# A two-block diffusion transformer on one core: modulation dealt out in single operations, w2 asked for earlier, a new order of the first steps

## The chip, the cores and the metric

The kernel runs on one core of a Trainium2 chip. The metric is the device time of one execution in microseconds (us), as the median of several. The core has a matrix engine (TensorE; in the profile PE for its products and PEld for its weight loads), a vector engine (VectorE, DVE), a scalar engine (ScalarE, ACT), GpSimd (POOL, unused here but for four constants) and SyncE (SP), which issues most of the DMA transfers. Each engine works through its own queue in order.

## The reference

256 latent tokens (`x`) and 256 context tokens (`ctx`), each 1024 wide, pass two blocks. Block 0 mixes by a short convolution, block 1 by grouped-query attention. Each block has an FFN, the mixer and a second FFN; each of the three reads a modulated norm and adds its gated result. The modulation vectors come from one product of `silu(c)` with a 1024 x 9216 matrix per block. Everything is fp32.

```python
def _modulate(t, g, shift, scale):
    return _rms(t, g) * (1 + scale) + shift

def _swiglu(h, w13, w2):
    gte, up = jnp.split(h @ w13, 2, axis=-1)
    return (jax.nn.silu(gte) * up) @ w2

for i in range(DEPTH):          # DEPTH = 2, FFN_HIDDEN = 2816
    mod = (silu(c) @ mod_w[i] + mod_b[i]).reshape(bsz, 3, 3, 1, D_MODEL)
    modc = (silu(c_ctx) @ mod_w[i] + mod_b[i]).reshape(3, 3, D_MODEL)
    lat = lat + 0.5 * mod[:, 0, 2] * _swiglu(_modulate(lat, norm_g[i, 0], mod[:, 0, 0], mod[:, 0, 1]),
                                             ffn_w13[i, 0], ffn_w2[i, 0])
    # the context the same way with modc; then the mixer (convolution or attention) on both,
    # gated by mod[:, 1, 2]; then the second FFN, gated by mod[:, 2, 2].
    # In block 1 the context only serves keys and values: its second FFN falls away.
```

## The kernel before

**Layout and arithmetic.** Activations lie transposed: 1024 features as 8 tiles (k) of 128 partitions, and 512 tokens as columns, the latents (s = 0) and the context (s = 1) with 256 each. Each operand is split into a high part that the matrix engine takes exactly and a low remainder (`split`, L90 to L92: ScalarE writes the high part, VectorE subtracts). `mm3` (L111) makes three products for one: high by high, high by low, low by high (lines L115, L116, L117).

**FFN.** `ffn` (L571) cuts the 22 tiles of the hidden width into thirds of 8, 7 and 7. For each hidden tile of a third a `Pair` (L496) computes gate and up with seven products of half size in place of eight (a Strassen scheme), which needs sums of the weights (VectorE) and sums of the activations, called T1 to T4 (`sums`). Then `project` (L433) multiplies the third's hidden tiles by w2 for 8 output tiles m, and `finish` (L412) adds each to x, times a gate. The first three tiles of a projection are begun before the last hidden tile is ready (`between`). After the last third, `tail_norm` computes the next norm. In the page the weight splits of w13 and w2 are `wh` and `wl`, the products of a pair `p` and `q`, those of a projection `py`.

**The modulation.** All but the first chapters of it are dot products on VectorE (L138, tile `junk`): one instruction multiplies a 128 x 1024 tile of the transposed matrix with one broadcast vector and sums it up. There are 72 chapters-by-quarters in all; `jobs` lists 64 blocks in the order in which they are wanted (chapter ch of block l, quarter `pair`). One `mod_job` loads 1 MB (`wr<-in_modT`) and runs four such instructions (two tiles by two vectors; two instructions for the last chapters of block 1, where the context is no longer read). `tick(share)` adds a share to `owed` and runs that many whole jobs; it is called after each `finish` in a projection (ev = 0.5, in the third FFN 0.9), and after each tile of the convolution (1.2). `mod_ready(l, ch)` runs at once whatever is missing for a chapter: a gate is asked for at a projection's first `finish` (`lazy_gate`), shift and scale at the norm behind the last tile, and everything left after the third FFN (L829), ahead of the q projections.

**What sets the order.** Nothing in the code is a queue of its own. A planner at build time takes the instructions in the order of the code as their priority, and puts on each engine the first one that is ready and has its buffers by its own estimate of the time; the order found is then fixed. Buffers that matter: three raw weight buffers of 1 MB (`wr`, L86), used by all weights and by the modulation alike; four pairs of split halves (`wh`, `wl`, L97); six PSUM tiles for products.

**The first block.** At the start nothing is there but x. `FIRST_STEPS` (L31) is a hand-written order of steps: W (load and split one w13 tile; three of them), P (`mod_pe`: a quarter of shift, ch 0, or scale, ch 1, of the first norm on TensorE from a separately laid out 1 MB of `mod0`), D (`mod_dve`: such a quarter on VectorE), S (load the broadcast vectors), N (the norm of two k tiles), M (the products of one w13 tile with two k tiles). Five quarters go through P and three through D. In a P step 8 products move 256 matrix columns past a 2-column stationary operand, the 2-row result is copied by ScalarE (L683), and two small products turn it (L685). Only after all steps come `h.sums()` and the three `w13_post` (silu, product, split).

Of the kernel before, what the change touches and what calls it, by code (L numbers as in the profile page):

```python
# [9 lines left out]
F32 = mybir.dt.float32  # L10
# [6 lines left out]
P = 128  # L17
# [20 lines left out]
def hybrid_kernel(ctx: ExitStack, tc: tile.TileContext, a: dict, out: bass.AP):  # L38
# [90 lines left out]
    def mod_job(l, ch, pair):  # L129
        mt = mod_tile(l, ch)  # L130
        nv = 1 if (l == 1 and ch >= 5) else 2
        raw = load_raw(a["modT"][l, ch * 4 + pair])
        for j in range(2):
            kt = pair * 2 + j
            col = ch * KT + kt
            for v in range(nv):
                junk = mp.tile([P, D], BF16, name=nm("junk"), tag="junk", bufs=1)
                nc.vector.tensor_tensor_reduce(  # L138
                    out=junk,
                    in0=raw[:, j * D : j * D + D],  # L140
                    in1=scbc[:, v, :],
                    scale=1.0,
                    scalar=modb[:, l, col : col + 1],
                    op0=ALU.mult,
                    op1=ALU.add,
                    accum_out=mt[:, kt, v : v + 1],
                )
        done[l, ch] += 1

    jobs = [(0, ch, p) for ch in range(2, 9) for p in range(4)]  # L150
    jobs += [(1, ch, p) for ch in range(9) for p in range(4)]
    owed = [0.0]

    def tick(share):

        owed[0] += share
        while jobs and owed[0] >= 1:
# [107 lines left out]
    class Blocks:  # L265
# [45 lines left out]
    class FirstBlocks(Blocks):  # L311
# [13 lines left out]
        def sums(self):  # L325
            r = self.raw
            tt = nc.vector.tensor_tensor
            for key in ("T1", "T2", "T3", "T4"):
                self.t[key] = hot("th"), hot("tl")
# [6 lines left out]
            b = lambda hf, s, q: r[2 * hf + q, s]  # L336
            for q in range(2):
# [779 lines left out]
```

## Time and profile before

| what | value |
|---|---|
| median of 3 runs | 1635.54 us (1632.44 to 1636.04) |
| the profiled execution's own time | 1636.17 us |
| its span, first to last instruction | 1634.1 us |
| mean granted TensorE clock | 0.984 of full |
| PE / PEld / DVE / ACT busy | 1581.4 / 1463.5 / 1358.5 / 735.1 us |
| modulation on VectorE (L138) | 236 instructions, 302.4 us |
| DMA | 248.81 MB, mean 152 GB/s |

The page gives for each engine its busy time and for groups of instructions the count, the mean duration and the idle time before them with what ended it. Queries of the trace give the same for any stretch of time, with the clock granted to TensorE in it (1.00 is full speed), the chain of work that ended last, and each queue's DMA issues. A busy TensorE isn't TensorE at its peak, so prices are taken from start to start or from counts in a stretch.

### The profile page before, as it was taken

The page shows a single profiled execution, that of the slowest core. Times are in us where ns is not written, and L with a number is a line of the kernel's source. Part 1 is how long each engine was busy: PE and PEld are TensorE (multiplying, and loading weights), DVE is VectorE, ACT ScalarE, POOL GpSimd, SP SyncE. Part 2 cuts the span into 40 slices and gives each one's busy share as a digit, 9 for nine tenths or more (in the row PEclk, how much of TensorE's full clock was granted, in tenths as well). Part 3 has the DMA queues.
Part 4 walks back from the last instruction along what each step waited for, and adds up shares of the span by engine and source line. Part 5 has one row for each costly group of instructions (what it writes and reads, how often), then busy time and mean ns, then how long its engine had stood idle before and what let it go on. Part 6 is the DMA issues. An engine that isn't in the chain of part 4 may idle for free.

```text
span 1634.1 us, 26052 instructions
## 1 busy us (share of the span) xinstructions
PE 1581.4 (97%) x10746; PEld 1463.5 (90%) x10746; DVE 1358.5 (83%) x2066; ACT 735.1 (45%) x1131; POOL 0.2 (0%) x4
## 2 busy tenths in 40 slices
PE   9898999999999999999999999989999989999999
PEld 6697898998888889989899889789899879899999
DVE  4999998889988979898898989999898978756454
ACT  5552352554322356435245465235255346554443
POOL 0000000000000000000000000000000000000000
PEclk9999999999999999999999999999999989999999
DMA  8335525334445513452433513552633742245453
GB/s 317 132 106 189 195 98 189 114 124 174 150 171 187 188 52 104 155 180 97 163 141 116 182 52 109 185 197 97 247 136 126 270 172 94 78 146 190 168 186 112
DMA packets 38279, 248.81 MB, mean 152 GB/s; under 512 B 5136, under 2 KB 6928, under 8 KB 12304
## 3 DMA queue, kind: packets, MB, share of 16 engines
q1 hardware_dynamic: 35712, 245.38, 42.9%
q10 hardware_dynamic: 2448, 1.76, 0.4%
q8 instruction: 84, 1.38, 0.3%
q14 instruction: 35, 0.29, 0.0%
HBM read 244.77 MB, written 1.05 MB: 150 GB/s over the span
## 4 chain that ended last, share of the span: by engine, by line
PE 85%; DVE 10%; DMA 2%; ACT 1%; issue 1%; DVEq 0%; ACTq 0%; SPq 0%
PE py L115 8%; PE py L117 8%; PE py L116 8%; PE p L117 7%; PE p L115 7%; PE p L116 7%; PE q L117 5%; PE q L115 5%; PE q L116 5%; DVE junk L138 4%; DVE wl L92 2%; PE pg L116 2%; PE pg L115 2%; PE pg L117 2%; PE pu L116 2%; PE pu L117 2%
## 5 line engine op out<-in xcount | busy, mean ns | idle before, releaser
L91 ACT ACTIVATE wh<-wr 128x1024 fp32r<-128x1024 f32 (+2 forms) x269 | 269.9, 1013 | 401.6 <-PE py L116 92.2
L92 DVE TENSOR_TENSOR wl<-wr,wh 128x1024 fp32r<-128x1024 f32 (+2 forms) x269 | 311.5, 1165 | 103.0 <-ACT wh L91 102.4
L138 DVE CUSTOM_DVE_ANT_0 junk<-wr,scbc,modb 128x1024 bf16<-128x1024 f32 x236 | 302.4, 1281 | 28.1 <-DMA wr<-in_modT 25.4
L117 PE MATMUL py<-gh,wl 128*128 128x512 f32 (+1 forms) x746 | 264.0, 355 | 5.9 <-DVE wl L92 5.9
L115 PE MATMUL py<-gh,wh 128*128 128x512 f32 (+1 forms) x746 | 265.2, 355 | 4.6 <-ACT wh L91 4.6
L116 PE MATMUL py<-gl,wh 128*128 128x512 f32 (+1 forms) x746 | 265.1, 355 | 0.0
L92 DVE TENSOR_TENSOR wl<-ws,wh 128x1024 fp32r<-128x1024 f32 x122 | 148.7, 1223 | 30.0 <-ACT wh L91 29.7
L117 PEld LDWEIGHTS py<-gh,wl 128*128 128x128 f32 x746 | 142.0, 190 | 26.7 <-DVE wl L92 7.3
L91 ACT ACTIVATE wh<-ws 128x1024 fp32r<-128x1024 f32 x122 | 128.3, 1058 | 81.9 <-PE p L116 37.6
L115 PEld LDWEIGHTS py<-gh,wh 128*128 128x128 f32 x746 | 142.3, 191 | 24.1 <-ACT wh L91 5.7
L116 PEld LDWEIGHTS py<-gl,wh 128*128 128x128 f32 x746 | 142.2, 191 | 18.3
L116 PE MATMUL p<-tl,wh 128*128 128x256 f32 x488 | 138.2, 283 | 0.0
L115 PE MATMUL p<-th,wh 128*128 128x256 f32 x488 | 138.2, 283 | 0.0
L117 PE MATMUL p<-th,wl 128*128 128x256 f32 x488 | 137.8, 283 | 0.0
L115 PE MATMUL q<-bh,wh 128*128 128x256 f32 x336 | 95.2, 283 | 0.4 <-ACT gm L551 0.4
L116 PE MATMUL q<-bl,wh 128*128 128x256 f32 x336 | 95.2, 283 | 0.0
L117 PE MATMUL q<-bh,wl 128*128 128x256 f32 x336 | 95.1, 283 | 0.0
L116 PEld LDWEIGHTS p<-tl,wh 128*128 128x128 f32 x488 | 93.8, 192 | 0.3
L115 PEld LDWEIGHTS p<-th,wh 128*128 128x128 f32 x488 | 93.8, 192 | 0.3
L117 PEld LDWEIGHTS p<-th,wl 128*128 128x128 f32 x488 | 93.5, 192 | 0.0
L417 DVE SCALAR_TENSOR_TENSOR x<-py,G,x 128x256 f32<-128x256 f32 x168 | 73.6, 479 | 22.0 <-PE py L117 21.7
L91 ACT ACTIVATE gh<-gm 128x512 fp32r<-128x512 f32 (+1 forms) x88 | 50.7, 576 | 62.7 <-DVE gm L568 52.9
(234 smaller groups left out, 4073.5 us busy)
## 6 DMA issues: line engine op xcount, KB each, us to landing
wr<-in_w SPq DMA_DIRECT2D x88, 1024.0 KB, 4.9
wr<-in_modT SPq DMA_DIRECT2D x67, 1024.0 KB, 5.0
wr<-in_w2b SPq DMA_DIRECT2D x32, 896.0 KB, 4.6
wr<-in_w2a SPq DMA_DIRECT2D x16, 1024.0 KB, 4.8
wr<-in_cw_cx SPq DMA_DIRECT2D x8, 1024.0 KB, 4.9
wr<-in_mod SPq DMA_DIRECT2D x5, 1024.0 KB, 7.9
wr<-in_cw_b SPq DMA_DIRECT2D x4, 1024.0 KB, 4.9
wr<-in_cw_out SPq DMA_DIRECT2D x4, 1024.0 KB, 5.0
```

The source lines that it names most:

```text
L91: nc.scalar.activation(out=hi, in_=src, func=AF.Copy)
L92: nc.vector.tensor_tensor(out=lo, in0=src, in1=hi.bitcast(F32), op=ALU.subtract)
L115: nc.tensor.matmul(ps, wh, mh, start=first, stop=False, **kw)
L116: nc.tensor.matmul(ps, wh, ml, start=False, stop=False, **kw)
L117: nc.tensor.matmul(ps, wl, mh, start=False, stop=last, **kw)
L138: nc.vector.tensor_tensor_reduce(out=junk, in0=raw[:, j * D : j * D + D], in1=scbc[:, v, :], scale=1.0, scalar=modb[:, l, col : col + 1], ...
L417: nc.vector.scalar_tensor_tensor(out=x[:, m, s * S : s * S + S], in0=ps[:, o : o + S], scalar=g[:, m, s : s + 1], in1=x[:, m, s * S : s * ...
```

## The change

1. `FIRST_STEPS` is reordered. All eight quarters of the first norm's modulation go through P; D is gone. P turns its product round: 128 x 128 pieces of the matrix are the stationary operand and the 2 columns of silu(c) are moved, so the result comes out in place, without the copy and the turning products. New steps: T (one of four parts of the activation sums, `part`), F (`w13_post` of one of the first three tiles), and U (one single modulation operation), eight of them.
2. A unit of the modulation is now one VectorE instruction (`mod_unit`); `next_unit` loads a new block when the last one's units are used up. `tick(n)` counts units: 1.5 per `finish` in the first two FFNs and in the fourth, where none is left, 2 in the third, 5 per tile of the convolution, 1 in its output projection; new is `ev13`, 1.6 after each pair in the first third of the first FFN. `mod_ready` fills up as before, in units.
3. In `project` each call for w2's tile m also asks for m + 1 and m + 2 (`get`).
4. `block(fine=True)` writes the high part straight from the norm and the low part from the same source; the fp32 copy comes after.

```diff
 FIRST_STEPS = (
-    "W0 P11 P10 P00 N0 P01 N1 P12 W1 S M00 M10 M01 M11 D02 N2 M02 D13 W2 D03 M12 M20 M21 N3 "
-    "M03 M22 M13 M23"
+    "P10 P00 W0 N0 P11 P01 N1 W1 S M00 M10 M01 P12 P02 M11 T0 W2 N2 M20 M02 P13 P03 M21 T1 M12 "
+    "N3 T2 M22 M03 F0 T3 M13 F1 U U U U M23 F2 U U U U"
 )
...
+    def next_unit():
+        if not units:
+            l, ch, pair = jobs.pop(0)
+            mod_tile(l, ch)
+            raw = load_raw(a["modT"][l, ch * 4 + pair])
+            units.extend(
+                (l, ch, pair, raw, j, v) for j in range(2) for v in range(streams(l, ch))
+            )
+        mod_unit(*units.pop(0))
+
+    def tick(n):
+
+        owed[0] += n
+        while (jobs or units) and owed[0] >= 1:
             owed[0] -= 1
-            mod_job(*jobs.pop(0))
+            next_unit()
 
     def mod_ready(l, ch):
-        while not ((l, ch) in done and done[l, ch] == 4):
-            mod_job(*jobs.pop(0))
+        while not ((l, ch) in done and done[l, ch] == 8 * streams(l, ch)):
+            next_unit()
         return modv[l, ch]
...
-                nc.scalar.activation(
-                    out=raw[:, c], in_=t, func=AF.Identity, bias=B[:, k, s : s + 1]
-                )
-                if fine and i % 2:
-                    c = slice((i - 1) * S, (i + 1) * S)
-                    split(hi[:, c], lo[:, c], raw[:, c])
+                b = B[:, k, s : s + 1]
+                if fine:
+                    nc.scalar.activation(out=hi[:, c], in_=t, func=AF.Identity, bias=b)
+                    nc.vector.scalar_tensor_tensor(
+                        out=lo[:, c], in0=t, scalar=b, in1=hi[:, c].bitcast(F32),
+                        op0=ALU.add, op1=ALU.subtract,
+                    )
+                nc.scalar.activation(out=raw[:, c], in_=t, func=AF.Identity, bias=b)
...
-        def sums(self):
+        def part(self, n):
...
+            q = n % 2
+            b11, b12, b21, b22 = (r.get((2 * hf + q, s)) for hf in range(2) for s in range(2))
+            if n < 2:
+                tt(out=b11, in0=b12, in1=b11, op=ALU.subtract)
+                keep("T1", q, b11)
+                return
+            tt(out=b12, in0=b22, in1=b12, op=ALU.add)
+            tt(out=b22, in0=b22, in1=b11, op=ALU.add)
+            keep("T2", q, b22)
+            tt(out=b21, in0=b21, in1=b22, op=ALU.subtract)
+            keep("T3", q, b12)
+            keep("T4", q, b21)
...
-        w2 = [ws(m) for m in range(nf)]
+        ahead = {}
+
+        def get(m):
+            for i in range(m, min(m + 3, KT)):
+                if i not in ahead:
+                    ahead[i] = ws(i)
+            return ahead[m]
+
+        w2 = [get(m) for m in range(nf)]
...
-    def ffn(l, b, h, tot, gate, tail, gs=(), ev=0.5):
+    def ffn(l, b, h, tot, gate, tail, gs=(), ev=1.5, ev13=0):
...
                     prev = pr
+                    if t == 0:
+                        tick(ev13)
...
-        for k in range(KT):
-            nc.tensor.matmul(
-                pr[:2, :S], sccol[:, k, :], raw[:, k * S : k * S + S],
-                start=(k == 0), stop=(k == KT - 1),
-            )
-        row = tp.tile([P, S], F32, name=nm("row"), tag="t", bufs=3)
-        nc.scalar.copy(row[:2, :], pr[:2, :S])
         for j in range(2):
-            nc.tensor.matmul(
-                pr[:, S + 2 * j : S + 2 * j + 2], row[:2, j * P : j * P + P], ident[:2, :2],
-                start=True, stop=True,
-            )
+            for k in range(KT):
+                o = k * S + j * P
+                nc.tensor.matmul(
+                    pr[:, 2 * j : 2 * j + 2], raw[:, o : o + P], sccol[:, k, :],
+                    start=(k == 0), stop=(k == KT - 1),
+                )
...
-    ffn(0, 0, h, T2, lazy_gate(0, 0), tail_norm(0, 1, hn), gs0)
+    ffn(0, 0, h, T2, lazy_gate(0, 0), tail_norm(0, 1, hn), gs0, 1.5, 1.6)
...
-        tick(1.2)
+        tick(5)
...
-        lazy_gate(0, 1), tail_norm(0, 2, hn), T2, 2, 0.5,
+        lazy_gate(0, 1), tail_norm(0, 2, hn), T2, 2, 1,
...
-    ffn(1, 0, h, T2, lazy_gate(1, 0), tail_norm(1, 1, hn), (), 0.9)
+    ffn(1, 0, h, T2, lazy_gate(1, 0), tail_norm(1, 1, hn), (), 2)
```

More of the change, by code (lines that the diff above doesn't have):

```diff
@@ L328, in sums @@
             for key in ("T1", "T2", "T3", "T4"):
-                self.t[key] = hot("th"), hot("tl")
+                if key not in self.t:
+                    self.t[key] = hot("th"), hot("tl")
             def keep(key, q, src):
@@ L462, in project @@
                 ready()
-            w = ws(m)
+            w = get(m)
             ps = psum("py")
@@ L468, in project @@
         if late:
-            wl = [ws(m) for m in (6, 7)]
+            wl = [get(m) for m in (6, 7)]
             if tail:
@@ L691, in mod_pe @@
             out=(A00 if ch else B00)[:, k2, :],
-            in0=pr[:, S : S + 4].rearrange("p (k v) -> p k v", v=2),
+            in0=pr[:, :4].rearrange("p (k v) -> p k v", v=2),
             in1=both(sb1[:, k2] if ch else modb[:, 0, k2]),
@@ L745, in hybrid_kernel @@
         steps[step[0]](*(int(c) for c in step[1:]))
-    done[0, 0] = done[0, 1] = 4
-    h = FirstBlocks(h, h32)
-    h.sums()
-    for i in range(3):
-        gs0.append(new_pair("g"))
-        w13_post(pps[i], gs0[i], 0, T2)
+    done[0, 0] = done[0, 1] = 16
+    h = hb
     convk = cload("convk", [P, 3, KT])
```

67 lines of the change are left out of this document (24 added, 43 removed).

## The prediction

> **What bounds the kernel now.** I read the page's totals first, then the granted clock and the busy time by stretches, then the chain of waits, and the DMA issues of SyncE's queue.
>
> ```profile
> span 1634.1 us, 26052 instructions
> PE 1581.4 (97%) x10746; PEld 1463.5 (90%) x10746; DVE 1358.5 (83%) x2066; ACT 735.1 (45%) x1131; POOL 0.2 (0%) x4
> wr<-in_modT SPq DMA_DIRECT2D x67, 1024.0 KB, 5.0
> ```
>
> TensorE is busy 97% of the span. A change can win only where TensorE waits or runs slowly, so I look for these places by stretches (us, then per engine busy time and instructions, then the clock granted):
>
> ```profile
> core 0: us, PE busy (x) PEld busy (x) DVE busy (x) ACT busy (x) POOL busy (x), PEclk, DMA share, GB/s
> 74.50:82.30 7.80, 2.79 (x15) 2.55 (x14) 7.80 (x12) 2.64 (x5) 0.00 (x0) 0.78 0.00 0
> 82.30:129.80 47.50, 47.50 (x385) 47.50 (x385) 42.28 (x52) 27.87 (x42) 0.00 (x0) 0.96 0.34 114
> 129.80:188.50 58.70, 51.53 (x231) 41.91 (x230) 56.68 (x93) 9.16 (x11) 0.00 (x0) 0.91 0.56 200
> 673.90:720.30 46.40, 46.40 (x217) 38.89 (x217) 46.15 (x74) 11.28 (x13) 0.00 (x0) 1.00 0.61 212
> 1027.90:1084.00 56.10, 49.19 (x223) 40.38 (x221) 55.03 (x91) 9.15 (x11) 0.00 (x0) 0.97 0.57 204
> 1300.00:1336.00 36.00, 27.44 (x170) 26.02 (x170) 30.73 (x62) 17.46 (x32) 0.00 (x0) 0.81 0.54 190
> 690.00:716.00 26.00, 26.00 (x116) 21.55 (x115) 25.86 (x42) 6.23 (x7) 0.00 (x0) 1.00 0.60 215
> 100.00:120.00 20.00, 20.00 (x169) 20.00 (x168) 18.79 (x25) 11.31 (x19) 0.00 (x0) 1.00 0.31 106
> ```
>
> The last two rows give TensorE's prices when nothing waits: 26/116 = 0.224 us for a product of 512 columns, 20/169 = 0.118 us for one of 256. The rows before show where it does wait: behind the first block (74.5 to 82.3), in the first w2 projection of the first and third FFN (58.7 and 56.1 us, where the same projection in the second FFN took 46.4), and around the first q projections (1300 to 1336). In the two slow projections VectorE is busy almost throughout, and this is with what (modulation operations alone):
>
> ```profile
> 129.80:188.50 58.70, 39.73 (x31) 0.91 0.56 200
> 673.90:720.30 46.40, 24.33 (x19) 1.00 0.61 212
> 1027.90:1084.00 56.10, 38.58 (x31) 0.97 0.57 204
> ```
>
> One single operation takes 24.33/19 = 1.28 us. With 19 of them a projection runs freely; 12 more cost 58.7 - 46.4 = 12.3 us in one place and 9.7 in the other, so about 0.8 to 1.0 us for each one above 20.
>
> **The modulation, counted from the code.** Before, the first projections get 32, 20 and 32 singles: forced at the first gate 4 blocks, 1 and 1 (a block is four singles on one 1 MB load), ticked 4, 4 and 7. After, 16 singles are done before the first FFN's projection (8 by U, 8 by the ticks of 1.6 in its pair loop), and the ticks then add 12, 40 in the convolution, 6 in its output projection. That leaves 96 where 112 are due at the second FFN's first gate: 16 are forced there, 12 ticked, 28 in all. At the third FFN 145 stand against 160: 15 forced (3 on a block already loaded), 16 ticked, so 28 on new loads. At the end 204 of 224 are done and 20 are forced, in 10 loads, because the last chapters use one stream; before it was 4 loads with 8.
>
> *First FFN's projection*: 12 singles, below 20, so it runs like 673.9: -12.3 us. *Second*: 8 above 20: 8 x 0.8 to 1.0 = +7 (from 0, if the slack behind 20 takes them, to 12, if the early w2 block also keeps a third raw buffer from the modulation, whose loads then queue behind it on SyncE, and with them the gate that the first finish reads; I take the rows' slope). *Third*: the same 28, against 9.7 lost now: -2.5 (from -9.7 to +3). *First FFN's pair loop*: VectorE has 1.2 us free in 20 (18.79 busy), about 0.6 in a pair of 10 us, and gets 1.6 x 1.28 = 2.0: five pairs lack 7 us. The projection that follows absorbs most: +2 (0 to 7).
>
> **The first block.** Before, a P step takes TensorE 4.1 us: 16 records of 256 columns and 4 that turn the row.
>
> ```profile
> 16.46 4.48 PE pr L678 x20
> 20.94 0.53 PE pr L685 x4
> 21.47 3.54 PE pr L678 x16
> ```
>
> After, a P step has 16 products, each with 128 columns of fp32 weights and 2 columns moved, which show as two records each, so 32. Such products are in the trace with one column, in the norm's sums (the first two rows, at clock 1.00) and in the attention's (the last two, at 0.50):
>
> ```profile
> 12.25 0.36 PE L212 MATMUL ss<-ones,sq 128*128 128x1 f32 x2
> ...
> 13.81 0.58 PE L223 MATMUL ss<-ident,ri 128*128 128x128 f32 x3
> 1327.02 1.70 PE L840 MATMUL pqs<-ones,sq 128*128 128x1 f32 x8
> 1328.58 0.77 PE L115 MATMUL pk<-hh,wh 128*128 128x512 f32 x1
> ```
>
> Between start and start these are 14 records in 1.56 us, 0.111 each, and 8 in 1.56 us, 0.195 each. A new P step is then 3.6 us at the full clock and 6.2 at half. Which one holds?
>
> ```profile
> 1324.74:1328.15 3.41, 3.41 (x18) 3.41 (x18) 3.41 (x8) 2.52 (x5) 0.00 (x0) 0.50 0.14 37
> 1328.15:1331.57 3.42, 3.42 (x13) 3.03 (x14) 3.42 (x8) 1.85 (x3) 0.00 (x0) 0.50 0.71 217
> 1331.57:1334.98 3.41, 3.41 (x30) 3.41 (x30) 3.20 (x6) 1.06 (x1) 0.00 (x0) 1.00 0.33 139
> 1433.97:1437.38 3.41, 1.54 (x10) 1.26 (x10) 2.07 (x5) 0.80 (x3) 0.00 (x0) 1.00 0.27 46
> 1437.38:1440.79 3.41, 2.77 (x13) 2.77 (x14) 3.41 (x10) 2.28 (x6) 0.00 (x0) 0.50 0.66 269
> ```
>
> In the first row TensorE is busy all 3.41 us and still isn't granted the full clock for the next 3.42; 1.1 us of that row are the one-column products. After the second row, nearly all wide products, it is granted. So a weight load with a column or two behind it seems not to count as work for the clock. A P step is nothing else, and four stand in a row at the start, two and two later. Against this speaks only that the clock stayed at 1.00 after the 1.56 us of such products at 12.25, but wide warm-up products filled the rest there. I take the half clock as likelier, two to one. The Trainium skill (TensorE: Matmul & The Clock Gate, Part 1) says that the clock falls after an idle stretch of about 3.4 us and follows how busy the engine is. Read as idle time alone, it keeps the new P steps at full clock, and the sum would be rival 1's 1631; the row at 1324.74, busy and not granted, does not agree with that reading.
>
> Sum to the end of the block's products: P starts at about 15 (the row at 13.81), not 16.5. At half clock some 2.7 of the 8 steps still run at full (the first, and the start of each later run): 2.7 x 3.6 + 5.3 x 6.2 = 42.6; 12 M steps of 12 products x 0.224 = 32.3; three restarts in which wide products run at half clock for a stretch, 2 us lost each: 6. The end is at 15 + 80.9 = 95.9. VectorE, 12 singles lighter there (15 us), has the pairs' weights by then, so the 7.8 us of mostly idle time at 74.5 go; pairs run from 95.9 where they ran freely from 82.3: **+13.6**. At full clock: 15 + 28.8 + 32.3 + about 1 waiting for a mod0 load = 77: -5. Five row copies on ScalarE and three tiny additions go, off the path. SyncE asks for eight mod0 blocks where it asked for five and three modT: the same bytes.
>
> **The end of the third FFN.** SyncE's queue there, before (issue, time over all, count):
>
> ```profile
> 1253.60 15.10 SPq L87 DMA_DIRECT2D wr<-in_modT  x4
> 1269.70 0.33 SPq L87 DMA_DIRECT2D wr<-in_w2b  x1
> 1272.23 4.70 SPq L87 DMA_DIRECT2D wr<-in_modT  x2
> 1286.92 0.33 SPq L87 DMA_DIRECT2D wr<-in_w2b  x1
> 1288.63 11.36 SPq L87 DMA_DIRECT2D wr<-in_modT  x4
> 1303.26 12.38 SPq L87 DMA_DIRECT2D wr<-in_wq  x2
> ```
>
> The q weights stand behind the last modulation loads, and the chain goes through them:
>
> ```profile
> 1303.26 5.68 DMA wr<-in_wq
> ...
> 1314.14 0.58 PE pq L117
> ```
>
> Six more loads at (11.36 - 0.33)/3 = 3.7 us are 22 us; the hole of 10 us before 1286.92 takes some 4 of it, since the w2 block is asked sooner. Wq lands 18 us later, at 1327, and the first q products start at 1328 in place of 1314. Of these 14 us some 8 come back: TensorE is busy only 27.4 of the 36 us to 1336, and the second wq, now 12 us behind the first, will follow at once. **+6** (0 if the loads find room in the projection, 16 if nothing comes back).
>
> **Edits taken at nothing.** W2 asked two tiles ahead: the planner already places a load as soon as a buffer is free, so it changes the order against the modulation loads only, counted above; between tiles VectorE's total decides, not w2. Without that cover it could win the longest wait for a w2 tile (total, times, longest), which lies in the first FFN's 12.3:
>
> ```profile
> PE py L115 <- ACT wh L91: 4.6, 1, 4.6
> ```
>
> The fine split writes hi at once and adds 0.5 us of ScalarE per operand beside running products: 0 (-2 to +2). T and F steps are the same instructions earlier; behind the last M they cost 7.8 us today, counted above.
>
> **Sum**, on the profiled execution's own 1636.2 us, which is 0.6 above the median of the three: first block +13.6, its projection -12.3, pair loop +2, second FFN +7, third -2.5, end +6: +13.8, so **1650**.
>
> **Rivals.** *1: the clock stays full in the P steps.* One mechanism, 18.6 us at the first block: 1650 - 18.6 = 1631, faster. It decides as soon as 13.8 of the 18.6 us don't come. For it: the clock after 12.25; against it: the row at 1324.74. *2: VectorE's forced singles find cover.* The planner brings them forward, second FFN +0, end +0, third -9.7: 1650 - 20 = 1630. Against it: singles need loads, and the three raw buffers hold pair weights until the last pair; for it: 20 cost nothing. *3: the q weights come later still, with nothing recovered*: 1650 + 10 = 1660. *4: the early w2 order isn't what the planner makes of it*: no time changes, since I priced it at none.
>
> **How the numbers follow.** Forecast with rival 4: 0.56, its own range 1638 to 1661. Rival 1: 0.28 (of it 0.18 faster, 0.05 the same, 0.05 slower, as the bursts cost). Rival 2: 0.06. Rival 3: 0.10. A change of 0.2% is about what a measurement of this kernel can tell. Faster: 0.18 + 0.06 = 0.24. Same: 0.05 + 0.03 of the forecast's low edge = 0.08. Slower: the rest, 0.68. The range reaches down to 1627, below rivals 1 and 2, and up to 1662.
>
> **What would show it.** Half clock granted between about 17 and 40 us, and P steps of 6 us there; the first products of the pair loop near 96; the first FFN's projection in 46 to 48 us with clock 1.00; idle TensorE at the end of the second FFN's first projection; wq issued near 1320 plus the shift. The prediction is wrong if the clock stays at 1.00 through the first 80 us, or if the second projection and the q weights show no longer waits.

## The result: 1697.1 us, 3.9% slower

The changed kernel takes 1697.12 us (median, 1694.58 to 1702.27) where the kernel before takes 1634.82; the ratio is 1.0387, with a 95% interval from 1.0358 to 1.0416. The forecast was 1650, at most 1662. The direction was right, the size was not.

The page of the changed kernel, its span and its totals:

```profile
span 1692.8 us, 26324 instructions
...
PE 1613.9 (95%) x10902; PEld 1504.7 (89%) x10902; DVE 1348.2 (80%) x2048; ACT 736.3 (43%) x1130; POOL 0.2 (0%) x4
...
PEclk6689999999999999989999999989999969999999
```

The span grew by 58.7 us, though VectorE is 10 us less busy. The clock row (40 slices of the span, tenths of full speed) has two deep holes: the first three slices and one at 1354 to 1396. The same stretches as in the forecast, now of the changed kernel (us, busy time and instructions of each engine, clock granted): the first block's products, the pair loop behind it, the first w2 projections of the first, second and third FFN, and the time ahead of the q products.

```profile
core 0: us, PE busy (x) PEld busy (x) DVE busy (x) ACT busy (x) POOL busy (x), PEclk, DMA share, GB/s
31.40:108.47 77.07, 74.29 (x337) 65.77 (x337) 33.62 (x69) 27.27 (x53) 0.00 (x0) 0.71 0.40 137
108.47:167.97 59.50, 51.25 (x397) 49.81 (x396) 59.33 (x83) 29.58 (x46) 0.00 (x0) 0.94 0.42 146
167.97:214.44 46.47, 46.47 (x218) 38.92 (x217) 40.85 (x62) 11.05 (x13) 0.00 (x0) 1.00 0.57 199
701.10:755.50 54.40, 49.85 (x218) 40.52 (x218) 49.39 (x81) 8.68 (x11) 0.00 (x0) 0.94 0.54 191
1066.40:1117.00 50.60, 48.39 (x219) 39.97 (x218) 45.38 (x76) 8.56 (x10) 0.00 (x0) 0.97 0.54 194
1340.00:1380.00 40.00, 9.06 (x52) 8.10 (x52) 38.82 (x78) 12.25 (x24) 0.00 (x0) 0.61 0.75 258
```

And the modulation's single operations in three of them:

```profile
701.10:755.50 54.40, 34.62 (x27) 0.94 0.54 191
1340.00:1380.00 40.00, 23.87 (x19) 0.61 0.75 258
167.97:214.44 46.47, 15.38 (x12) 1.00 0.57 199
```

The first FFN's projection (167.97) runs freely with 12 singles, as forecast. The second FFN's (701.10) has 27 and loses time. At 1340 TensorE works 9 us of 40, at a clock of 0.61, while VectorE is busy 38.8 us, 23.9 of them with singles.

The shift of the same products between the two traces (start after minus start before) shows where the 58.7 us arise; beside it what the forecast's terms give for that place:

| place | forecast | measured |
|---|---|---|
| first product of the first w2 projection | +15.6 | +38.1 |
| behind that projection | +3.3 | +25.9 |
| second FFN, start of the first projection | +3.3 | +27.2 |
| second FFN, start of the second projection | +10.3 | +39.8 |
| third FFN, start of the last projection | +7.8 | +38.6 |
| first product of the attention scores | +13.8 | +58.8 |
| last product | +13.8 | +58.6 |

Three places lose more than was thought: the first block with its pair loop (22.5 us more), the second FFN (5.6 more, and only half of the 2.5 comes back in the third), and the end of the third FFN (14.2 more).

**The first block, read in the trace.** TensorE's queue at the start (start, us, line, output and operands, count, idle time before it and who ended it):

```profile
13.91 13.26 PE L704 MATMUL pr<-sccol,wr 128*128 128x2 f32 x64
31.40 0.80 PE L116 MATMUL pg<-hh,wh 128*128 128x512 f32 x1 [4.23 <-ACT wh L92]
...
33.27 6.82 PE L704 MATMUL pr<-sccol,wr 128*128 128x2 f32 x32
...
40.53 0.63 PE L118 MATMUL pu<-hh,wl 128*128 128x512 f32 x1
40.95 0.63 PE L116 MATMUL pg<-hh,wh 128*128 128x512 f32 x1
```

Two P steps (64 records) take 13.26 us without a gap, and the clock granted falls to half at 14.47 and comes back at 55.43. The wide products in between cost 0.42 us from start to start, not 0.224. Counted so over the first block as a whole (13.91 to 108.47), the P steps take 45.1 us, the 144 wide products 42.5, idle time 7.0.

The fall itself is not the work of the new P: it comes 0.56 us after the first P product. In e7, one of the runs below, the P steps are the old ones and start at 16.93; there the clock falls at 14.50 too, but it is back as soon as P's wide products have filled a stretch (by the columns above):

```profile
14.50:17.91 3.41, 0.98 (x3) 0.37 (x4) 2.58 (x4) 2.36 (x6) 0.00 (x0) 0.50 0.88 334
17.91:21.32 3.41, 3.41 (x10) 1.03 (x8) 0.00 (x0) 0.00 (x0) 0.00 (x0) 0.50 0.85 293
21.32:24.73 3.41, 3.41 (x19) 1.51 (x17) 0.33 (x2) 0.36 (x1) 0.00 (x0) 1.00 0.45 132
```

What the new P does is to keep the clock down.

**The pair loop.** Behind the block's last product TensorE waits once for 6.3 us, for the low half of a weight that VectorE writes. The longest of TensorE's waits from 104 to 128 us (engine, line, waited for, total, times, longest):

```profile
PE p L118 <- DVE wl L93: 6.3, 1, 6.3
```

What VectorE did meanwhile, until it wrote `wl` (start, us, line, output and operands):

```profile
111.12 1.28 DVE L136 CUSTOM_DVE_ANT_0 junk<-wr,scbc,modb 128x1024 bf16<-128x1024 f32 x1
...
112.93 1.28 DVE L136 CUSTOM_DVE_ANT_0 junk<-wr,scbc,modb 128x1024 bf16<-128x1024 f32 x1
...
114.14 1.23 DVE L93 TENSOR_TENSOR wl<-wr,wh 128x1024 fp32r<-128x1024 f32 x1
```

The singles of the U steps stand in front of the weight that TensorE waits for.

**The end of the third FFN.** SyncE's queue there (issue, time over all, count):

```profile
1317.04 0.33 SPq L88 DMA_DIRECT2D wr<-in_w2b  x1
1322.58 45.56 SPq L88 DMA_DIRECT2D wr<-in_modT  x12
1371.01 3.53 SPq L88 DMA_DIRECT2D wr<-in_wq  x2
```

The chain that ended last, in order of time (start, us, piece):

```profile
1374.58 1.20 DVE junk L136
1376.08 1.29 DVE junk L136
1377.38 1.15 DVE wl L93
1378.58 0.58 PE pq L118
```

Twelve modulation loads stand ahead of the q weights, and the last singles ahead of the first q weight's low half. It is not the loads themselves that set their distance of 4 us. From 1320 to 1372 SyncE waits most of the time for a single on VectorE (L136) that still reads the raw buffer (who waited for whom, total, times, longest):

```profile
SPq L88 <- DVE mod L136: 42.9, 11, 10.0
```

So the queue goes at VectorE's pace. Wq is asked for at 1371.0; with the shift of 38.6 that stood before this place it would have been 1341.9.

### The profile page after: what moved, and what is told of

The parts are those of the page before. It is cut to its first block, busy times and chain, and to the rows that moved or that the text cites. A ratio compares the mean times of both kernels' runs of the same rounds, so it can differ in the third digit from the quotient of the medians.

```text
span 1692.8 us, 26324 instructions
## 1 busy us (share of the span) xinstructions
PE 1613.9 (95%) x10902; PEld 1504.7 (89%) x10902; DVE 1348.2 (80%) x2048; ACT 736.3 (43%) x1130; POOL 0.2 (0%) x4
## 4 chain that ended last, share of the span: by engine, by line
PE 88%; DVE 9%; ACT 2%; issue 1%; DVEq 0%; ACTq 0%
PE py L118 9%; PE py L116 9%; PE py L117 9%; PE p L118 7%; PE p L116 7%; PE p L117 7%; PE q L118 5%; PE q L116 5%; PE q L117 5%; DVE junk L136 4%; PE pr L704 3%; PE pg L116 2%; PE pg L117 2%; PE pu L117 2%; PE pu L118 2%; PE pu L116 2%
## 5 line engine op out<-in xcount | busy, mean ns | idle before, releaser
L136 DVE CUSTOM_DVE_ANT_0 junk<-wr,scbc,modb 128x1024 bf16<-128x1024 f32 x224 | 287.3, 1282 | 17.8 <-DMA wr<-in_modT 15.7
L93 DVE TENSOR_TENSOR wl<-ws,wh 128x1024 fp32r<-128x1024 f32 x122 | 149.0, 1223 | 30.2 <-ACT wh L92 30.1
L116 PEld LDWEIGHTS py<-gh,wh 128*128 128x128 f32 x746 | 142.3, 191 | 21.1 <-ACT wh L92 2.5
```

The costliest lines, as they stand in the source:

```text
L93: nc.vector.tensor_tensor(out=lo, in0=src, in1=hi.bitcast(F32), op=ALU.subtract)
L116: nc.tensor.matmul(ps, wh, mh, start=first, stop=False, **kw)
L136: nc.vector.tensor_tensor_reduce(out=junk, in0=raw[:, j * D : j * D + D], in1=scbc[:, v, :], scale=1.0, scalar=modb[:, l, col : col + 1], ...
```

## The experiments

Times are medians in us. Each row also has the shift of the same products against the kernel before, from the profiles, at the places used above.

| run | us | first w2 projection | behind it | second FFN, first projection | its second projection | third FFN, last projection | scores |
|---|---|---|---|---|---|---|---|
| the changed kernel | 1697.1 | +38.1 | +25.9 | +27.2 | +39.8 | +38.6 | +58.8 |
| e1_old_p | 1671.2 | +7.7 | -4.5 | -2.8 | +9.9 | +15.7 | +35.8 |
| e2_first_old | 1667.5 | +9.9 | -2.3 | -0.2 | +12.8 | +13.7 | +34.7 |
| e3_dealt | 1664.1 | +40.4 | +28.2 | +30.1 | +30.1 | +38.0 | +28.7 |
| e4_no_ahead | 1690.6 | +38.7 | +26.5 | +27.5 | +37.5 | +34.1 | +52.5 |
| e5_filler | 1681.6 | +27.1 | +14.9 | +16.6 | +29.3 | +26.7 | +47.5 |
| e6_old_p_dealt | 1615.2 | +4.2 | -8.0 | -6.4 | -6.4 | -10.8 | -21.7 |
| e7_before_dealt | 1621.6 | +0.8 | -5.3 | -0.5 | -0.5 | -2.7 | -12.3 |
| e8_one_load | 1688.2 | +37.0 | +24.8 | +26.0 | +39.8 | +41.1 | +53.6 |
| e9_no_last | 1664.0 | +43.2 | +31.0 | +32.2 | +44.8 | +43.7 | +31.2 |
| e10_before_new_p | 1651.4 | +16.4 | +16.3 | +16.2 | +16.2 | +15.9 | +15.5 |
| e11_dealt_ahead | 1630.9 | +5.2 | -7.0 | -4.9 | -4.9 | +3.0 | -7.7 |
| e12_no_u | 1678.1 | +29.0 | +18.1 | +20.1 | +21.1 | +22.6 | +42.4 |
| e13_best_no_u | 1611.3 | +5.1 | -7.0 | -6.7 | -6.7 | -8.6 | -22.2 |
| e14_old_fine | 1696.1 | +37.3 | +25.1 | +26.0 | +38.9 | +39.0 | +58.6 |

### e1: the old P step

```diff
-        for j in range(2):
-            for k in range(KT):
-                o = k * S + j * P
-                nc.tensor.matmul(pr[:, 2 * j : 2 * j + 2], raw[:, o : o + P], sccol[:, k, :], ...)
+        for k in range(KT):
+            nc.tensor.matmul(pr[:2, :S], sccol[:, k, :], raw[:, k * S : k * S + S], ...)
+        row = tp.tile([P, S], F32, name=nm("row"), tag="t", bufs=3)
+        nc.scalar.copy(row[:2, :], pr[:2, :S])
+        for j in range(2):
+            nc.tensor.matmul(pr[:, S + 2 * j : S + 2 * j + 2], row[:2, j * P : j * P + P], ident[:2, :2], ...)
```

> The changed kernel with one edit undone: a P step is the old one again (2-column stationary operand, 256 matrix columns moved, the row copied and turned). Order of the steps, U, T, F and all dealing stay. Theory 1 (the new form of P costs time at half clock and leaves the next products cold): the clock stays at 1.00 from 17 to 60 us, a P step takes about 4.1 us in place of 6.4, no wide products run cold, the first product of the pair loop comes at 84 to 90 us where the changed kernel has 108.5; about 1677 us. Rival (the block waits for its loads, each mod0 load behind a raw buffer that a P step frees): the pair loop still begins later than 100, 1690 or more.

1671.2 us (ratio to before 1.0226, 1.021 to 1.0243). The pair loop begins at 84.3, the first w2 projection 30.4 us sooner than in the changed kernel. The block and the pair loop of this run:

```profile
13.86:84.25 70.39, 68.97 (x309) 41.88 (x309) 45.43 (x92) 35.33 (x72) 0.00 (x0) 0.98 0.60 217
84.25:137.60 53.35, 50.54 (x398) 49.40 (x397) 51.47 (x70) 29.06 (x45) 0.00 (x0) 0.97 0.37 134
```

The clock is 0.98 in the block, and the wide products take 33.9 us where they took 42.5. So the form of P is the largest part of the block's loss, and the loads aren't: they follow the P steps that free their buffers. With the old P, the new order and the dealing together leave the kernel 4.5 us ahead of the one before once the first w2 projection is over.

### e2: the first block as before

```diff
-    "P10 P00 W0 N0 P11 P01 N1 W1 S M00 M10 M01 P12 P02 M11 T0 W2 N2 M20 M02 P13 P03 M21 T1 M12 "
-    "N3 T2 M22 M03 F0 T3 M13 F1 U U U U M23 F2 U U U U"
+    "W0 P11 P10 P00 N0 P01 N1 P12 W1 S M00 M10 M01 M11 D02 N2 M02 D13 W2 D03 M12 M20 M21 N3 "
+    "M03 M22 M13 M23 T0 T1 T2 T3 F0 F1 F2 U U U U U U U U"
```

Beside it the old P and the three D steps.

> The changed kernel with the old order of the first steps, the old P and the three D steps; T, F and the eight U follow behind the last M step, so that the count of singles dealt later is that of the changed kernel. Theory 1 (the first block's order and its P steps carry the +38 us at the pair loop): the pair loop begins within 5 us of the kernel before, the first products of the w2 projection come 5 to 15 us late in place of 38 (the eight U and the ticks of 1.6 load VectorE in the pair loop); 1664 to 1675. Rival (the U and the ticks in the pair loop carry most of it): the w2 projection still begins 25 us late or more, 1685 or more.

1667.5 us. The pair loop begins as in the kernel before (74.8), and the w2 projection +9.9 late, with 16 singles in the pair loop. The projection gives back 12.2 for it. This run has the old P, as e1 has, so it doesn't tell the form of P from the order. Beside e1 it says that the old order on top of the old P is worth only another 3.7 us.

### e3: no forced singles

```diff
-    ffn(0, 0, h, T2, lazy_gate(0, 0), tail_norm(0, 1, hn), gs0, 1.5, 1.6)
+    ffn(0, 0, h, T2, lazy_gate(0, 0), tail_norm(0, 1, hn), gs0, 2, 1.6)
-        tick(5)
+        tick(6)
-    ffn(0, 1, h, T2, lazy_gate(0, 2), tail_norm(1, 0, hn), ())
+    ffn(0, 1, h, T2, lazy_gate(0, 2), tail_norm(1, 0, hn), (), 2.5)
-    ffn(1, 0, h, T2, lazy_gate(1, 0), tail_norm(1, 1, hn), (), 2)
+    ffn(1, 0, h, T2, lazy_gate(1, 0), tail_norm(1, 1, hn), (), 2.5)
```

> The changed kernel with higher ticks, so that no single is forced at the second and third FFN's first gate nor ahead of the q projections: 2 per finish in the first FFN (1.5 before), 6 per tile of the convolution (5), 2.5 in the second and third FFN (1.5 and 2). Theory 1 (the forced singles, 28 in the second FFN's first projection and 20 in 10 loads ahead of the q weights, carry the +12.6 and the +20.3): the second projection gives back 8 to 12, the end 12 to 20, the third FFN 0 to 8; 1660 to 1677. Rival (w2 asked two tiles ahead holds the third raw buffer, and the modulation and the q weights wait for it): both delays stay, 1690 or more.

1664.1 us. The second FFN's projection (704.00) and the time ahead of the q products (1300.20):

```profile
704.00:750.40 46.40, 46.40 (x218) 38.88 (x217) 42.19 (x67) 11.32 (x13) 0.00 (x0) 1.00 0.50 181
1300.20:1345.60 45.40, 44.29 (x256) 38.95 (x254) 39.74 (x75) 17.53 (x27) 0.00 (x0) 1.00 0.68 247
```

The second projection loses nothing (+30.1 on both sides of it), and the end gives back 9.3 where it cost 20.2. So both delays need the forced singles. A part of the gain is lost again between them: +7.9 from the second FFN's second projection to the third FFN's last.

### e4: w2 one tile at a time

```diff
-            for i in range(m, min(m + 3, KT)):
+            for i in (m,):
```

> The changed kernel with w2's tiles asked for one at a time as before. Theory 1 (forced singles): within 3 us of the changed kernel, 1694 to 1700. Rival (the early w2 loads hold the third raw buffer): the second FFN's first projection and the q weights come 5 to 15 us sooner each, 1667 to 1687.

1690.6 us, 6.6 less than the changed kernel and between the two theories. The second FFN's projection still loses 10.0 (12.6 with w2 ahead), and the third FFN's first projection gives 3.8 (+38.5 to +34.7) where with w2 ahead it loses 0.8 (+38.4 to +39.2). So the forced singles make most of the delay, and asking ahead adds to it. e11 looks at how.

### e5: extra wide products in the new P

```diff
+            for _ in range(4):
+                nc.tensor.matmul(pr[:, S:], ones, x[:, 0, :S], start=True, stop=True)
```

> The changed kernel with work added: behind each eight of the new P step's products stand four extra products of 256 moved fp32 columns that nobody reads, 64 in all, which cost 0.44 us each by the old P step's records (3.54 us for 16 records, two a product), 28 us together. Theory 1 (the clock falls in the new P steps because products of two columns do not count as work, and rises and holds where wide products fill half of the time): the clock is 1.00 from 17 us to the end of the block, a P step takes about 3.6 + 3.5 = 7.1 us, the wide products of the M steps run at 0.224 us each, and although 28 us of work are added the pair loop begins within 8 us of the changed kernel's 108.5; 1690 to 1706. Rival (the clock falls for another reason, or it is not the clock that costs): half clock stays, the pair loop begins at 136 or later, 1724 or more.

1681.6 us: the kernel does some 30 us of useless products more (128 records, from start to start) and is 15.5 us faster. Its stretches until and after 21.11 us, by the same columns as above:

```profile
14.29:21.11 6.82, 6.82 (x27) 6.10 (x26) 0.00 (x0) 2.56 (x5) 0.00 (x0) 0.50 0.48 183
21.11:95.00 73.89, 73.89 (x455) 67.12 (x454) 36.34 (x78) 23.03 (x48) 0.00 (x0) 1.00 0.51 185
```

The first rows of its P steps in TensorE's queue (L704 the narrow products, L709 the extra ones):

```profile
14.14 3.40 PE L704 MATMUL pr<-sccol,wr 128*128 128x2 f32 x16
17.41 3.76 PE L709 MATMUL pr<-x,ones 128*128 128x256 f32 x8
20.96 1.92 PE L704 MATMUL pr<-sccol,wr 128*128 128x2 f32 x16
```

The first sixteen narrow records take 3.40 us at half clock, later ones 1.92 and less. After one stretch with wide products the clock rises and stays at 1.00. Work was only added, so it is the clock that costs, and what keeps it up is wide products, not a busy engine. Without the extra ones, the block's P steps take 28.9 us here (45.1 in the changed kernel), its wide products 33.3 (42.5), and idle time is 0 (7.0). The run went beyond theory 1: the pair loop begins 2.0 us sooner, and its own wait is gone too, 9 us more by the w2 projection. The U are still in this kernel, but here all eight singles start between 73.7 and 100.2, before the block ends at 106.4; in the changed kernel five of the eight start behind its end. So the U cost where they are bunched behind the block. Why they come sooner here isn't separated: the extra products also change the order that the planner makes.

### e6: the old P, higher ticks, w2 one at a time

The edits of e1, e3 and e4 together.

> The changed kernel with three edits at once: the old P step, the higher ticks, w2's tiles asked for one at a time. The new order of the first steps, T, F, U, the dealing in single operations and the fine split stay. Theory 1 (the three losses lie in different stages and add): 1697.1 - 25.9 - 33.0 - 6.6 = 1631.6, 1627 to 1637. Rival (they share a cause, VectorE's total or the third raw buffer, so that the second one undone finds less): 1640 or more.

1615.2 us: ratio to before 0.9885 (0.9871 to 0.99), faster than both kernels and 16 us better than the three gains added. e11 accounts for 9 of these 16: w2 ahead costs 15.7 us here, where e4 put 6.6 on it. The first block, the first projections of three FFNs, and the time ahead of the q products:

```profile
15.00:82.00 67.00, 66.03 (x302) 40.62 (x300) 45.57 (x92) 34.64 (x70) 0.00 (x0) 1.00 0.60 222
...
134.00:180.50 46.50, 46.50 (x218) 38.95 (x217) 45.23 (x70) 11.43 (x13) 0.00 (x0) 1.00 0.62 226
667.40:713.90 46.50, 46.50 (x219) 38.95 (x217) 45.31 (x71) 11.28 (x13) 0.00 (x0) 1.00 0.56 203
1026.50:1073.00 46.50, 46.50 (x219) 38.95 (x218) 44.78 (x69) 11.17 (x14) 0.00 (x0) 1.00 0.56 201
1296.00:1336.00 40.00, 39.21 (x273) 35.83 (x272) 29.91 (x56) 22.61 (x38) 0.00 (x0) 1.00 0.35 109
```

All three projections take 46.5 us with TensorE busy throughout, where the kernel before paid 58.7, 46.4 and 56.1. The dealing in single operations is worth having, as e7 shows without the new order; it is the new P, too few ticks and the early w2 that cost. What the new order is worth isn't separated: e1 is 3.7 us slower than e2 with the old order, e6 6.4 us faster than e7, and each pair differs in its singles too.

### e7: the first block of before, single dealing

```diff
-    ffn(0, 0, h, T2, lazy_gate(0, 0), tail_norm(0, 1, hn), gs0, 1.5, 1.6)
+    ffn(0, 0, h, T2, lazy_gate(0, 0), tail_norm(0, 1, hn), gs0, (0.5, 2.5, 2.5))
```

Beside it the old order, P and D, the ticks of e3 with 2 per finish in the convolution's output projection, and w2 one tile at a time.

> The first block as in the kernel before (order, P, D, no U, no ticks in the pair loop) with single dealing so that little is forced: 16 forced and 4 ticked in the first FFN's first projection, 2.5 per finish in its other two and in the second and third FFN, 6 per tile of the convolution, 2 in its output projection; w2 one tile at a time. Theory 1 (single dealing is of use where a projection then holds 20 singles in place of 32): the first FFN's projection gives 10 to 12, the third FFN and the end 2 to 8; 1614 to 1626, faster than the kernel before. Rival (a projection loses by any single, wherever it stands): 1632 or more.

1621.6 us, ratio 0.9924 (0.991 to 0.9939). Single dealing alone makes the kernel faster. The first FFN's projection gives 6.1 of the 10 to 12 expected, the end 9.6.

### e8 and e9: what stands ahead of the q weights

```diff
 e8
-            raw = load_raw(a["modT"][l, ch * 4 + pair])
+            raw = again[0] if again else load_raw(a["modT"][l, ch * 4 + pair])
+            if last[0]:
+                again[:] = [raw]
...
+    last[0] = True
     mod_ready(1, 8)
 e9
-    mod_ready(1, 8)
+    for ch in range(9):
+        if done.get((1, ch), 0) < 8 * streams(1, ch):
+            nc.vector.memset(mod_tile(1, ch), 0.0)
+            done[1, ch] = 8 * streams(1, ch)
+    jobs.clear()
+    units.clear()
```

> The changed kernel, but the 20 singles forced ahead of the q projections all read one loaded block in place of ten, so that these chapters hold wrong values; VectorE's work is the same, nine loads of 1 MB are left out. Theory 1 (the ten loads hold the q weights back on SyncE's queue): the first q products come 12 to 20 us sooner, 1677 to 1685. Rival (the 20 singles delay the norm on VectorE, whose operations alternate with them from 1350 to 1370): they come at most 6 us sooner, 1691 or more.

> The changed kernel without the last 20 singles and their ten loads (those chapters are set to zero, so the output is not the reference's). With one load in place of ten the run before came 8.9 us sooner; this one takes VectorE's part away too. Theory 1 (loads and singles both stand ahead of the q products, and the 20 singles are the larger part): another 12 to 22 us, 1666 to 1676. Rival (what is left there belongs to the norm and the weight splits, not to the singles): at most 4 us below the run with one load, 1684 or more.

With nine loads less: 1688.2 us, 8.9 less. With neither loads nor singles: 1664.0, 33.1 less. In shifts from the third FFN's last projection to the scores: +20.2 in the changed kernel, +12.5 in e8, -12.5 in e9. So the nine loads are 7.7 us of it, and the 20 singles with the one load that is left 25.0, which is about 20 times a single's own 1.28 us. The order in which they were taken out may shift some of it from one to the other. In e8 the first q products do come 30.7 us sooner, but then TensorE waits for VectorE elsewhere. The stretch in e8, in two parts:

```profile
1340.00:1360.00 20.00, 13.23 (x84) 12.34 (x83) 19.60 (x40) 9.11 (x18) 0.00 (x0) 0.77 0.23 81
1360.00:1380.00 20.00, 12.03 (x94) 11.65 (x92) 18.95 (x34) 6.82 (x10) 0.00 (x0) 0.84 0.25 97
```

Its longest wait there:

```profile
PE pk L118 <- DVE wl L93: 14.1, 1, 14.1
```

The same two parts in e9:

```profile
1340.00:1360.00 20.00, 18.28 (x148) 17.52 (x147) 16.23 (x36) 11.37 (x21) 0.00 (x0) 1.00 0.55 208
1360.00:1380.00 20.00, 20.00 (x128) 18.03 (x127) 14.16 (x27) 11.78 (x20) 0.00 (x0) 1.00 0.50 164
```

Neither of e8's theories holds alone, and the one that I began with, the loads, is the smaller part. In e8 VectorE is full (19.60 of 20), and a weight's low half stands behind the singles; without them TensorE works through.

### e10: the new P alone, in the kernel before

The first diff above the other way round, in the kernel before.

> The kernel before with the new form of P alone, five steps in the old order. Theory 1 (the form costs by the clock): half clock from about 17 us on, a P step takes 6.4 us in place of 4.1, 11.5 us for five and some 2 us for each restart in which wide products run cold; the pair loop begins 10 to 16 us late, and a part of it is lost in VectorE's backlog behind the block: 1641 to 1652. Rival (the backlog on VectorE behind the block takes it up): 1637 or less.

1651.4 us, ratio 1.0102 (1.0077 to 1.0127). The first three P steps in TensorE's queue:

```profile
15.82 20.13 PE L680 MATMUL pr<-sccol,wr 128*128 128x2 f32 x96 [1.12 <-DMA wr<-in_mod]
```

The stretch from there, with the clock granted:

```profile
16.35:50.48 34.13, 32.54 (x139) 31.11 (x139) 8.85 (x24) 6.46 (x17) 0.00 (x0) 0.50 0.53 192
```

Three steps (96 records) take 20.13 us, where before a step took 4.1; the clock is 0.50 until 50.48. The w2 projection begins 16.4 us late and nothing later gives it back. The backlog behind the block doesn't take it up.

### e11: asking ahead where nothing is forced

e6 with `get` as in the change.

> The kernel with the old P and the higher ticks, but with w2 asked two tiles ahead as in the change. It tells whether asking ahead costs by itself. Theory 1 (it costs only where forced modulation loads want the third raw buffer at the same time): 1612 to 1619, as with one tile at a time (1615.2). Rival (it costs the 6.6 us that it cost in the changed kernel, wherever it is): 1620 to 1624. Or it helps where nothing is forced: 1611 or less.

1630.9 us: asking two tiles ahead costs 15.7 us here, more than either theory said. Of the 13.8 us that it has lost against e6 at the third FFN's last projection, 12.3 arise after the start of the second FFN's second one. At the first of the places TensorE waits for a pair weight:

```profile
PE q L116 <- ACT wh L92: 3.4, 1, 3.4
```

The second weight of that pair loop is asked for at 822.8 us; in e6 it was asked for at 812.7. Between the projection's last w2 load and the first weight of the pair loop stand three modulation loads in e11 and one in e6. So w2 asked for early pushes modulation loads behind itself, and these push the pair weights. This was read at the one place; the rest of the 15.7 us was not worked out.

### e12 and e13: without the U

```diff
-    "N3 T2 M22 M03 F0 T3 M13 F1 U U U U M23 F2 U U U U"
+    "N3 T2 M22 M03 F0 T3 M13 F1 M23 F2"
```

In e12 with 2 per finish in the convolution's output projection; e13 is e6 with this edit and ticks of 1.5, 2 and 2 in the first FFN's projections.

> The changed kernel without the eight U; its eight singles are forced at the first FFN's first gate (8 forced and 12 ticked there, 20 in all), and the output projection of the convolution deals 2 in place of 1 per finish, so that the count behind it stays nearly the same. Theory 1 (the two loads of the U stand ahead of the pair loop's weights and make the 6.6 us of idle time behind the block): that gap goes, the w2 projection begins 6 to 12 us sooner than the changed kernel's, of which the projection keeps most; 1685 to 1692. Rival (the gap is VectorE's backlog of sums, silu and weight splits, late with the half clock): the w2 projection begins at most 3 us sooner, 1694 or more.

> The old P, the higher ticks, w2 one tile at a time (1615.2 with the U), now without the eight U; 8 singles are forced at the first FFN's first gate, 1.5 per finish there, 2 in its other projections, 2 in the convolution's output projection. Theory 1 (the U delay the pair weights on VectorE wherever they stand, 9 us in the changed kernel): the w2 projection begins 5 to 9 us sooner, and the time is 1606 to 1611. Rival (they only cost where the block ends late and VectorE's work is bunched behind it, as with the half clock): 1613 to 1618.

e12 takes 1678.1 us. The pair loop takes 9.3 us less than in the changed kernel (59.50), and the wait of 6.3 is gone:

```profile
108.71:158.90 50.19, 48.85 (x398) 47.88 (x397) 49.97 (x68) 28.73 (x45) 0.00 (x0) 1.00 0.39 132
```

The rest of its gain lies in the second FFN, where 20 singles are left and it loses 1.0 in place of 12.6:

```profile
693.90:741.40 47.50, 25.61 (x20) 1.00 0.53 193
```

e12's first theory named the U's loads. The trace of the changed kernel shows their singles on VectorE in front of `wl`; loads and singles weren't taken apart here. e13 takes 1611.3 us, ratio 0.9858 (0.9838 to 0.9878), against e6's 0.9885 (0.9871 to 0.99): the intervals meet. Its pair loop is 4.5 us shorter than e6's but begins 5.4 later, since the planner orders the block otherwise. So its w2 projection starts 0.9 us later than e6's and not 5 to 9 sooner, as theory 1 had it. The U cost in the pair loop there too, and it isn't settled what they are worth in all.

### e14: the old fine split

```diff
-                if fine:
-                    nc.scalar.activation(out=hi[:, c], in_=t, func=AF.Identity, bias=b)
-                    nc.vector.scalar_tensor_tensor(out=lo[:, c], in0=t, scalar=b, ...)
-                nc.scalar.activation(out=raw[:, c], in_=t, func=AF.Identity, bias=b)
+                nc.scalar.activation(out=raw[:, c], in_=t, func=AF.Identity, bias=B[:, k, s : s + 1])
+                if fine and i % 2:
+                    c = slice((i - 1) * S, (i + 1) * S)
+                    split(hi[:, c], lo[:, c], raw[:, c])
```

> The changed kernel with the old fine split (fp32 copy first, high and low part from it, two tiles at a time). The forecast put this edit at nothing, with -2 to +2: 1695 to 1699. Rival (writing the high part at once, with the fp32 copy behind, holds up the sums of the activations in the second and third FFN): 1691 or less.

1696.1 us, within the spread of the changed kernel: the fine split is worth nothing, as it was put.

## Why the prediction came out too low

**The first block (+13.6): the mechanism was right, the size was not.** The clock was half from 14.5 to 55.4, as forecast; e5 and e10 show that it is the clock. The term's parts, from 13.91: P steps 42.6 forecast, 45.1 measured; wide products with their restarts 38.3 and 42.5, since the three stretches at half clock in the block (14.47 to 55.43, 65.67 to 79.32, 89.56 to 96.39) cost them more than 2 us each; idle time 0 and 7.0, of which 4.2 is a wait for a weight's high half before the first product and the rest stands between P steps and products. That makes the block end at 108.5 in place of 95.9. The 2 us for a restart was an estimate without a row; by the 42.5 it is 3.4 each.

**"The 7.8 us of mostly idle time at 74.5 go".** This step failed. A wait of 6.3 us stands behind the block's last product in the changed kernel. I had counted VectorE 12 singles lighter in the block and forgotten that the eight U put singles at that very place, ahead of the pair weights. e12 takes the U out, and the wait goes; in e5 it goes with the U in place, since they come before the block's end. The **pair loop (+2)** was mis-sized by the same: it takes 59.5 us where the sum gave it 49.6 (from 95.9 to 129.85 + 15.6); 9.3 of these 10 us go without the U.

**First FFN's projection (-12.3): right.** 12 singles, 46.47 us, clock 1.00; the shift falls by 12.2.

**Second FFN (+7): mis-sized, inside its own bounds but for 0.6.** 28 singles cost 12.6. e4 gives 10.0 without w2 ahead, e12 1.0 with 20 singles and w2 ahead. From 20 singles to 28 that is 1.5 us for each with w2 ahead and, by e4's 10.0 above the same 1.0, some 1.1 without it: about a single's own time of 1.28, where I took 0.8 to 1.0.

**Third FFN (-2.5): +0.8**, within its bounds. Without w2 ahead it is -3.8, so the count of singles was priced well and the early w2 took the gain.

**W2 two tiles ahead, "taken at nothing": failed.** That VectorE's total decides, and not the order of the loads, did not hold. The edit costs 6.6 us in the changed kernel (2.6 in the second FFN's first projection, 4.6 in the third's) and 15.7 where nothing is forced. The one wait looked at (e11) is for a pair weight that was asked for 10 us later than in e6, behind modulation loads that the early w2 had pushed back; three raw buffers serve them all. Rival 4, by which no time changes, fell with it.

**The end of the third FFN (+6): failed, it is +20.2.** "Wq lands 18 us later" is the step that failed: wq is asked for 29 us later. There are eight more modulation loads and not six, 4.1 us apart (45.56 us for twelve) and not 3.7. And these distances, which I took for the price of a load, are mostly SyncE's waits for singles on VectorE: 42.9 us of the changed kernel's queue. The q products start again 25.8 us late against the shift of 38.6, where I had 14; of this 5.6 come back, where I had 8. I priced loads alone and left out the 20 singles, which e8 and e9 price at 25.0 us (with one load) against 7.7 for nine loads: they stand on VectorE among the norm and the weights' low halves. TensorE, idle meanwhile, drops to half clock from 1349 to 1383.

**The rivals.** Rival 1, the full clock, is refuted by the clock in the rows. Its price of 18.6 us was too low: in e5, where the clock is up, the same P steps and wide products take 25.4 us less and idle time 7.0 less. Rival 2, no cost in the second FFN and at the end, fell by 12.6 and 20.2 us. Rival 3, the q weights later still with nothing recovered, was the nearest and got 1 in 10; it too fell short.

Three of the errors are alike: behind the first block, in the second FFN and at the end of the third, singles were priced as if VectorE had time for them there, and it had little (59.3 us busy of 59.5, 49.4 of 54.4, 38.8 of 40). e12, e3 and e9 show it by taking the singles away.

## What to carry to other kernels

A busy TensorE isn't a warm one: before a product is turned round so that the big operand is the stationary one, count the moved columns, and if these are few, expect half clock, also for the wide products right behind it. When work on a nearly full engine is dealt out finer, count what is still due at each place that forces it, and price the engine's time for every piece above the free time at its whole duration, beside that of the loads. A load asked for early isn't free where buffers are shared: name who has the buffer now. And a distance between two loads in a queue isn't a load's price before you know what the queue waited for.

## What the runs showed of the hardware

- 64 records of two moved columns in a row ran for 13.26 us without a gap, from 13.91 on. The clock was at 0.50 from 14.47 and stayed there until 55.43. The Trainium skill (TensorE: Matmul & The Clock Gate, Part 1) has the clock at full after about 3.4 us of sustained work and at half after an idle stretch of that length. These rows do not agree with it: from 14.47 to 27.17 the engine was busy all the time and had half the clock. Part 4 of the same page of the Trainium skill says of transposes that they don't count as busy in the same way. No run here tests that, but they show another kind of work of which the same holds.
- Wide fp32 products in half of the time were enough: in e5 the clock was 1.00 from 21.11 to 95.00, narrow records cost 0.11 us each (16 in 1.84) in place of 0.21 (64 in 13.26), and a kernel with 30 us more work was 15.5 us faster.
- In e6 the clock is 1.00 in every stretch shown, and the whole kernel takes 1.2% less than before.
